# A hybrid layer (gated DeltaNet, RG-LRU, SwiGLU) in fp32 on one core: another order of the start, of the decay and of the recurrent steps

## The chip, the cores and the metric

One core of one Trainium2 chip. The metric is the device time of one execution in microseconds, the median of several runs. The kernel works in fp32 throughout; there is one launch.

## What is computed

```python
proj = x @ w_in                                   # x: 512 x 1024, 8720 columns
q, k, v, z, b_raw, a_raw, lru_x, lru_g, gate_dn, gate_lru = jnp.split(proj, IN_SPLIT_IDX, axis=-1)
qkv = jax.nn.silu(causal_depthwise_conv(jnp.concatenate([q, k, v], axis=-1), dn_conv_w))
...
beta = jax.nn.sigmoid(b_raw.astype(jnp.float32))
g = -jnp.exp(dn_A_log) * jax.nn.softplus(a_raw + dn_dt_bias)
o = gated_delta_rule_chunked(q, k, v, g, beta)    # 8 heads of 128, chunks, a triangular solve per chunk
...
u = causal_depthwise_conv(lru_x, lru_conv_w) + lru_conv_b
h = rg_lru(u, lru_w_a, lru_b_a, lru_w_i, lru_b_i, lru_lambda)     # 10 blocks of 128
y_lru = (h * jax.nn.gelu(lru_g)) @ w_branch_lru
merged = g_dn * y_dn + g_lru * y_lru
return merged @ w_out
```

Behind it follow a residual with layer norm, a SwiGLU with 2816 hidden columns, and a second residual with layer norm.

## The kernel before

Every large product is made of three matmuls of 512 columns (mm3, L154): weights and data are split into a high and a low part, and high x high, high x low and low x high are added in PSUM. The high part is a cast on ACT, the low part a subtraction on DVE or GpSimd (split, L129; split_w, L173). Weights come in pieces of 128 columns over 8 blocks of 128 rows (load_w, L164, on SP's queue), so one piece is 24 matmuls. The projections are called pj (q, k, v, z), lx and lg (LRU input and gate) and g (merge gates).

**Start** (L184 to L280). SP loads x (tiles xc) and the first weights (tiles wk, columns of k and q of heads 0 and 1). ACT's queue issues the load of wba (the columns of b_raw and a_raw) and eight loads of small parameters into rw. PE transposes the blocks of x (xp, L245); ACT and DVE split them into xT. psba is the product for beta and the decay, 16 columns wide. `first` are the four products of the first weights, made behind all transposes and all of psba. ACT and DVE are in the written order there; afterwards a scheduler orders them, and `urgent()` (L96) raises the priority of what stands in it.

**Recurrence.** Four chains dn_chain (L475), one for two heads each, run between the projections. Their steps, by the names of their PSUM tiles: kt (k to token order), kk (k times k), qt, qk, vt, then the inversion of the triangular matrices on 16 x 16 to 128 x 128 blocks (m, and i in several steps; xa, Fl and Yf are its tiles, most of its work is on DVE), then per chunk ks, xr, su, and the outputs oa, ob. Five chains lru_chain (L802) make the gates of the LRU (lw, L807) and the recurrence: r and ig are its gates, a the factor, u the state, gl the gelu of lg. decay_chain (L349) makes beta and the cumulated decay from psba; through it every dn_chain must wait.

**What sets the order.** PE's order is written by a planner at build time. It has a clock that only counts PE's own work, and a table LAT (L23) of how long the other engines need behind each step:

```python
                    pe, lat = next(ch[1])
                    ch[0] = clock[0] + pe + lat
                    clock[0] += pe
```

advance (L290) takes a chain's next step once the clock is past ch[0]; otherwise the next three matmuls of a projection are issued. before_merge (L848) takes projections in the sequence ORDER, as soon as enough of 40 SBUF slots are free (slot, free, NEED, and room, L436, which makes a chain wait for slots). PSUM has eight banks in two rings (bank, L85): "d", five banks after the start, for the chains, and "p" for projections. A chain step takes the bank that was taken five takes earlier, and waits on the chip until that one's reader is done. conv (L423) reads a projection's bank with one pass on ACT and three on DVE.

**The end.** merge, w_out, a layer norm, the SwiGLU and its down product follow. The last product (L1205ff) has its blocks' banks in `tops`; `cc` are banks that the combined products used, and dl0 is a further bank of ring "p", which the sum into h read just before.

Of the kernel before, what the change touches and what calls it, by code (L numbers as in the profile page):

```python
# [22 lines left out]
LAT = {  # L23
    "F": 13.0, "kt": 12.0, "q": 5.2, "qk": 5.0, "P": 4.0, "vt": 2.0, "u": 10.0, "sub": 33.0, "m1": 7.0,
    "m2": 8.0, "i2": 6.0, "i4": 7.0, "i5": 7.0, "x": 8.0, "ks": 5.0, "xr": 7.0, "su": 6.5, "ot": 26.0,
    "ba": 9.0, "g": 2.5, "conv": 14.0,
}
# [6 lines left out]
P = 128  # L34
# [12 lines left out]
def layer_kernel(  # L47
# [159 lines left out]
    load_x(256, 256)  # L207
    load_x(512, 256)
    load_x(768, 256)
    for m in range(4):  # L210
        load_first(m)

# [3 lines left out]
    S.dma_start(out=wbav, in_=win[:, :, CB:CB + 16])  # L216
    rw = slot("rw")
    r1, r2 = rw[0:96, 0, 0:P], rw[0:97, 1, 0:P]
    S.dma_start(out=r1, in_=dn_conv_w[0].rearrange("k (n p) -> (k n) p", p=P))
    S.dma_start(out=r2[0:40, :], in_=lru_conv_w[0].rearrange("k (n p) -> (k n) p", p=P))  # L220
    for j, v in enumerate((lru_conv_b, lru_b_a, lru_b_i, lru_lambda)):
        S.dma_start(out=r2[40 + 10 * j:50 + 10 * j, :], in_=v[0].rearrange("(n p) -> n p", p=P))
    S.dma_start(out=r2[80:96, :], in_=b_merge_gate[0].rearrange("(n p) -> n p", p=P))
    S.dma_start(out=r2[96:97, :], in_=dn_norm_w)
# [25 lines left out]
    def split_first(m, j):  # L250
        if j == 0:
            ws.append([wp.tile([P, 1024], F32R, tag=t, name=f"{t}f{m}") for t in ("wh", "wl")])
        split(*[t[:, T * j:T * j + T] for t in ws[m]], wk[m][:, j], V if m % 2 == 0 else G)
        if j == 1:
            free(wk[m])
# [6 lines left out]

    with tc.manual_schedule(engines={mybir.EngineType.Activation, mybir.EngineType.DVE}):
        for k in range(NK):
            transpose_x(k)
            if k == 1:
                n = NK * 16
                split(wbh[:, 0, 0:n], wbh[:, 1, 0:n], wba[:, 0, 0:n])
            if k >= 2:
                product_ba(k - 2)  # L270
            if k >= 6:
                split_first(0, k - 6)
        product_ba(6)
        product_ba(7)
    for t in xcs:
        free(t)
# [44 lines left out]
    def start(gen, lat):  # L321
        chains.append([clock[0] + lat, gen])

    def softplus(o, v, tmp):

        e, s2 = tmp
        act(e, v, AF.Abs)
        act(e, e, AF.Exp, scale=-1.0)
        V.tensor_scalar(out=s2, in0=e, scalar1=2.0, scalar2=None, op0=ALU.add)
        V.reciprocal(out=s2, in_=s2)  # L330
        tt(V, e, e, s2, ALU.mult)
        tt(V, s2, e, e, ALU.mult)
# [16 lines left out]
    def decay_chain():  # L349
# [452 lines left out]
    def lru_chain(p, u, r, ig, gw):  # L802
        n0 = 2 * p
        for g, (t, b) in enumerate(((r, 1), (ig, 2))):
# [8 lines left out]
        a, gl = slot(f"a{p}"), slot(f"gl{p}")  # L813
        gls[p] = gl
# [6 lines left out]
        stt(m, m, 1.0, r, ALU.add, ALU.mult)  # L821
        act(m, m, AF.Sqrt, bias=tiny)
# [9 lines left out]
        free(r, a, gl, ig)  # L832
# [38 lines left out]
    for n in range(4 * NK):  # L871

        k, i = (n // 4, n % 4) if n < 24 else (6 + n % 2, (n - 24) // 2)
        if n % 8 == 0 and n < 24:
            split_first(n // 8 + 1, 0)
            split_first(n // 8 + 1, 1)
        if n == 8:
            columns_of_parameters()
        wh, wl = [t.rearrange("p (j k c) -> p j k c", j=2, k=2) for t in ws[k // 2]]
        cs = slice((i % 2) * P, (i % 2) * P + P)  # L880
        mm3(first[i], wh[:, i // 2, k % 2, cs], wl[:, i // 2, k % 2, cs], xT[k][:, 0], xT[k][:, 1],
            k == 0, k == NK - 1)
        clock[0] += 0.68
        advance()
# [320 lines left out]
    for q, (name, right, banks, new, then) in enumerate(products):  # L1205
# [62 lines left out]
```

## Time and profile before

| | |
|---|---|
| median of three runs (lowest, highest) | 1018.65 us (1018.27, 1019.77) |
| the profiled execution, its own time and its span | 1017.21 us, 1015.5 us |
| PE busy, share of the span | 985.5 us, 97% |
| PE weight loads | 810.5 us, 80% |
| DVE | 621.8 us, 61% |
| ACT | 451.3 us, 44% |
| GpSimd (POOL) | 268.7 us, 26% |
| DMA | 128.52 MB, mean 127 GB/s |

The shares are means over the span: the DVE has 61% of it, but it is busy nearly all the time in some slices of the recurrence and little in others. Names like kt<-ident,x in the rows give the tile written and the tiles read, without their numbers; PEld is the load of weights into PE, which goes beside its matmuls. The trace lists a wait under the line of the instruction that waited, and behind the arrow what ended it.

### The profile page before, as it was taken

How to read it: one execution, taken by the hardware profiler on the slowest of the kernel's cores; microseconds unless marked ns; L12 is line 12 of the kernel's file. 1: busy time of each engine (PE TensorE's matmuls, PEld its weight loads, DVE VectorE, ACT ScalarE, POOL GpSimd, SP SyncE). 2: the span in 40 equal slices, each digit the busy share in tenths (PEclk: the TensorE clock that was granted, in tenths of full speed). 3: DMA queues.
4: the chain of work that ended last, by engine and by line, in shares of the span. 5: the costliest groups of instructions: out<-in, count | busy, mean ns of one | idle time of the engine just before them, and what ended most of it. 6: DMA issues, size and time to landing. Idle time of an engine off the chain costs nothing.

```text
span 1015.5 us, 14361 instructions
## 1 busy us (share of the span) xinstructions
PE 985.5 (97%) x5531; PEld 810.5 (80%) x5531; DVE 621.8 (61%) x1318; ACT 451.3 (44%) x619; POOL 268.7 (26%) x278
## 2 busy tenths in 40 slices
PE   7999999999999999999999999999999999999986
PEld 4887767777887888788888888798888888888875
DVE  3678999846777791265223464976344443388676
ACT  4598365359416743574322234322222222375451
POOL 2473534425343724265200003132000100000041
PEclk9999999999999999999999999999999999999998
DMA  8331322323222223234332527579354563346653
GB/s 255 105 104 53 84 74 63 84 73 84 64 63 73 75 66 89 63 112 127 103 94 84 171 88 207 187 268 327 110 163 154 181 207 90 97 136 195 194 188 107
DMA packets 161288, 128.52 MB, mean 127 GB/s; under 512 B 5499, under 2 KB 140860, under 8 KB 161220
## 3 DMA queue, kind: packets, MB, share of 16 engines
q1 hardware_dynamic: 152032, 99.12, 33.3%
q0 software_dynamic: 7872, 28.32, 7.5%
q8 instruction: 43, 0.70, 0.3%
q10 hardware_dynamic: 1316, 0.16, 0.1%
q14 instruction: 25, 0.20, 0.1%
HBM read 113.94 MB, written 13.65 MB: 126 GB/s over the span
## 4 chain that ended last, share of the span: by engine, by line
PE 75%; DVE 14%; ACT 4%; POOL 2%; issue 2%; DMA 1%; ACTq 0%; DVEq 0%; POOLq 0%
PE fu L157 4%; PE fg L157 4%; PE fg L155 4%; PE fu L155 4%; PE fu L156 4%; PE fg L156 4%; PE pj L155 3%; PE pj L156 3%; PE pj L157 3%; PE g L155 3%; PE g L157 3%; PE g L156 3%; DVE xa L121 3%; PE yl L157 2%; PE yl L156 2%
## 5 line engine op out<-in xcount | busy, mean ns | idle before, releaser
L135 ACT CAST wh<-wr 128x1024 fp32r<-128x1024 f32 (+1 forms) x163 | 168.5, 1034 | 363.2 <-PE fg L156 74.3
L121 POOL TENSOR_TENSOR wl<-wr,wh 128x512 fp32r<-128x512 f32 x128 | 172.4, 1369 | 216.0 <-ACT wh L135 211.5
L121 DVE TENSOR_TENSOR wl<-wr,wh 128x1024 fp32r<-128x1024 f32 x99 | 120.1, 1215 | 113.0 <-ACT wh L135 112.9
L155 PE MATMUL pj<-xT,wh 128*128 128x512 f32 x224 | 91.9, 410 | 0.0
L157 PE MATMUL pj<-xT,wl 128*128 128x512 f32 x224 | 87.5, 391 | 0.0
L156 PE MATMUL pj<-xT,wh 128*128 128x512 f32 x224 | 87.4, 390 | 0.0
L127 ACT ACT_TABLE_LOAD x62 | 79.5, 1283 | 12.4 <-DMA rw<-in_lru_conv_w 6.9
L155 PE MATMUL fg<-hk,wh 128*128 128x512 f32 x160 | 62.3, 389 | 0.0
L156 PE MATMUL fg<-hk,wh 128*128 128x512 f32 x160 | 62.3, 389 | 0.0
L157 PE MATMUL fg<-hk,wl 128*128 128x512 f32 x160 | 62.2, 389 | 0.0
L155 PE MATMUL fu<-hk,wh 128*128 128x512 f32 x160 | 62.2, 389 | 0.0
L156 PE MATMUL fu<-hk,wh 128*128 128x512 f32 x160 | 62.2, 389 | 0.0
L157 PE MATMUL fu<-hk,wl 128*128 128x512 f32 x160 | 62.2, 389 | 0.0
L155 PE MATMUL g<-xT,wh 128*128 128x512 f32 x128 | 51.1, 399 | 0.0
L157 PE MATMUL g<-xT,wl 128*128 128x512 f32 x128 | 50.0, 391 | 0.0
L156 PE MATMUL g<-xT,wh 128*128 128x512 f32 x128 | 49.9, 390 | 0.0
L124 DVE SCALAR_TENSOR_TENSOR x<-pj,cols,x 128x511 f32<-128x511 f32 (+2 forms) x60 | 44.5, 742 | 8.6 <-ACT x L127 8.2
L157 PEld LDWEIGHTS pj<-xT,wl 128*128 128x128 f32 x224 | 42.0, 188 | 9.1
L155 PEld LDWEIGHTS pj<-xT,wh 128*128 128x128 f32 x224 | 42.1, 188 | 7.9
L121 POOL TENSOR_TENSOR h<-h,g 128x512 f32<-128x512 f32 x4 | 6.0, 1499 | 160.2 <-ACT h L127 160.2
L156 PEld LDWEIGHTS pj<-xT,wh 128*128 128x128 f32 x224 | 42.2, 188 | 7.1
L121 DVE TENSOR_TENSOR xa<-xa 128x16 f32<-128x16 f32 (+14 forms) x116 | 37.6, 324 | 2.3
(387 smaller groups left out, 2366.2 us busy)
## 6 DMA issues: line engine op xcount, KB each, us to landing
wr<-in_w_in SPq DMA_DIRECT2D x64, 512.0 KB, 3.6
wr<-in_w_ffn_gate SPq DMA_DIRECT2D x22, 512.0 KB, 3.7
wr<-in_w_ffn_up SPq DMA_DIRECT2D x22, 512.0 KB, 3.7
b<-in_w_ffn_down POOLq DMA_DIRECT2D x22, 512.0 KB, 5.2
td<-b POOLq DMA_DIRECT2D x22, 512.0 KB, 4.0
wr<-td SPq DMA_DIRECT2D x20, 512.0 KB, 3.7
wr<-in_w_ffn_down SPq DMA_DIRECT2D x15, 512.0 KB, 3.4
wr<-in_w_branch_lru SPq DMA_DIRECT2D x8, 512.0 KB, 3.4
```

The lines of the kernel that those rows point to most:

```text
L121: return eng.tensor_tensor(out=o, in0=a, in1=b, op=op)
L124: return V.scalar_tensor_tensor(out=o, in0=a, scalar=s, in1=b, op0=op0, op1=op1)
L127: return S.activation(out=o, in_=i, func=func, **kw)
L135: S.copy(out=hi, in_=src)
L155: PE.matmul(ps, wh, rh, start=start, stop=False, **kw)
L156: PE.matmul(ps, wh, rl, start=False, stop=False, **kw)
L157: PE.matmul(ps, wl, rh, start=False, stop=stop, **kw)
```

## The change

Five parts. (1) SP's queue alternates blocks of x and first weights; the eight small loads go from ACT's queue to SP's, behind them. In the start PE makes, for each block of x, the transposes, then the previous block's psba product and its four first products; all low parts of the first weights are made on DVE. (2) beta comes from an exponential, an addition and a reciprocal instead of the sigmoid, the absolute value in softplus from DVE; the decay's operations have high priority. (3) lru_chain takes its slots r, ig and a when its gates begin, and waits for room then; gl takes r's place. (4) Thirteen planned latencies are longer. (5) The last product's first block has the bank cc[0].

```diff
-    "F": 13.0, "kt": 12.0, "q": 5.2, "qk": 5.0, "P": 4.0, "vt": 2.0, "u": 10.0, "sub": 33.0, "m1": 7.0,
-    "m2": 8.0, "i2": 6.0, "i4": 7.0, "i5": 7.0, "x": 8.0, "ks": 5.0, "xr": 7.0, "su": 6.5, "ot": 26.0,
-    "ba": 9.0, "g": 2.5, "conv": 14.0,
+    "F": 13.0, "kt": 13.5, "q": 5.2, "qk": 5.5, "P": 4.5, "vt": 2.0, "u": 10.0, "sub": 33.0, "m1": 8.5,
+    "m2": 9.5, "i2": 7.0, "i4": 7.5, "i5": 7.5, "x": 8.5, "ks": 6.0, "xr": 7.5, "su": 7.0, "ot": 26.0,
+    "ba": 13.0, "g": 2.5, "conv": 14.0,
...
-    load_x(256, 256)
-    load_x(512, 256)
-    load_x(768, 256)
-    for m in range(4):
-        load_first(m)
-
     wba, wbh = slot("wba"), slot("wbah", F32R)
     wbav = wba[:, 0, 0:NK * 16].rearrange("p (k c) -> p k c", c=16)
     wbhv = wbh[:, :, 0:NK * 16].rearrange("p s (k c) -> p s k c", c=16)
     S.dma_start(out=wbav, in_=win[:, :, CB:CB + 16])
+    load_first(0)
+    for m in range(1, 4):
+        load_x(256 * m, 256)
+        load_first(m)
...
-    S.dma_start(out=r1, in_=dn_conv_w[0].rearrange("k (n p) -> (k n) p", p=P))
-    S.dma_start(out=r2[0:40, :], in_=lru_conv_w[0].rearrange("k (n p) -> (k n) p", p=P))
+    nc.sync.dma_start(out=r1, in_=dn_conv_w[0].rearrange("k (n p) -> (k n) p", p=P))
+    nc.sync.dma_start(out=r2[0:40, :], in_=lru_conv_w[0].rearrange("k (n p) -> (k n) p", p=P))
...
-        split(*[t[:, T * j:T * j + T] for t in ws[m]], wk[m][:, j], V if m % 2 == 0 else G)
+        split(*[t[:, T * j:T * j + T] for t in ws[m]], wk[m][:, j])
...
+        transpose_x(0)
+        n = NK * 16
+        split(wbh[:, 0, 0:n], wbh[:, 1, 0:n], wba[:, 0, 0:n])
+        for k in range(1, NK):
             transpose_x(k)
-            if k == 1:
-                n = NK * 16
-                split(wbh[:, 0, 0:n], wbh[:, 1, 0:n], wba[:, 0, 0:n])
-            if k >= 2:
-                product_ba(k - 2)
-            if k >= 6:
-                split_first(0, k - 6)
-        product_ba(6)
-        product_ba(7)
-    for t in xcs:
-        free(t)
+            if k % 2 == 1:
+                split_first(k // 2, 0)
+                split_first(k // 2, 1)
+                free(xcs[k // 2])
+            product_ba(k - 1)
+            for i in range(4 if k < NK - 1 else 0):
+                product_first(k - 1, i)
+        product_ba(NK - 1)
...
-        act(e, v, AF.Abs)
+        stt(e, v, -1.0, v, ALU.mult, ALU.max)
...
-        act(beta, psb3[:, :, 0:8], AF.Sigmoid)
-        tt(V, ga, psb3[:, :, 8:16], dtb[:, None, :].to_broadcast([P, 4, H]), ALU.add)
-        softplus(gg, ga, (e1, e2))
-        act(nA, nA, AF.Exp)
-        stt(gg, gg, -1.0, nA[:, None, :].to_broadcast([P, 4, H]), ALU.mult, ALU.mult)
+        with urgent():
+            tt(V, ga, psb3[:, :, 8:16], dtb[:, None, :].to_broadcast([P, 4, H]), ALU.add)
+            softplus(gg, ga, (e1, e2))
+            act(nA, nA, AF.Exp)
+            stt(gg, gg, -1.0, nA[:, None, :].to_broadcast([P, 4, H]), ALU.mult, ALU.mult)
+
+            act(beta, psb3[:, :, 0:8], AF.Exp, scale=-1.0)
+            V.tensor_scalar(out=beta, in0=beta, scalar1=1.0, scalar2=3e38, op0=ALU.add, op1=ALU.min)
+            V.reciprocal(out=beta, in_=beta)
...
-    def lru_chain(p, u, r, ig, gw):
+    def lru_chain(p, u, gw):
         n0 = 2 * p
+        yield from room(3)
+        r, ig, a = slot(f"r{p}"), slot(f"ig{p}"), slot(f"a{p}")
...
-        a, gl = slot(f"a{p}"), slot(f"gl{p}")
-        gls[p] = gl
...
+        gls[p] = gl = r
...
-    for n in range(4 * NK):
-
-        k, i = (n // 4, n % 4) if n < 24 else (6 + n % 2, (n - 24) // 2)
-        if n % 8 == 0 and n < 24:
-            split_first(n // 8 + 1, 0)
-            split_first(n // 8 + 1, 1)
-        if n == 8:
-            columns_of_parameters()
-        wh, wl = [t.rearrange("p (j k c) -> p j k c", j=2, k=2) for t in ws[k // 2]]
-        cs = slice((i % 2) * P, (i % 2) * P + P)
-        mm3(first[i], wh[:, i // 2, k % 2, cs], wl[:, i // 2, k % 2, cs], xT[k][:, 0], xT[k][:, 1],
-            k == 0, k == NK - 1)
-        clock[0] += 0.68
-        advance()
+    columns_of_parameters()
+
+    for i in range(4):
+        for k in (6, 7):
+            product_first(k, i)
+            clock[0] += 0.68
+            advance()
...
-            tops = [[(0, bankp("dl0"))], [(0, bankd("dl1")[:, 0:256]), (256, bankd("dl2")[:, 0:256])]]
+            tops = [[(0, cc[0])], [(0, bankd("dl1")[:, 0:256]), (256, bankd("dl2")[:, 0:256])]]
```

product_first(k, i) is the body of the removed loop: mm3 into first[i] with the weights of block k.

What moves, first on **ACT, at the start** (whf are high parts of the first weights, wbah those of wba, nA a parameter of the decay). Before:

```order
L223 DMA rw<-in_b_merge_gate 16x128
L224 DMA rw<-in_dn_norm_w 1x128
L127 ACT_TABLE_LOAD
L127 ACTIVATE nA<-nA 128x8
L130 CAST xT_132<-xp_127 128x512
L130 CAST xT_140<-xp_135 128x512
L130 CAST wbah<-wba 128x128
L130 CAST xT_150<-xp_145 128x512
L130 CAST xT_161<-xp_156 128x512
L130 CAST xT_172<-xp_167 128x512
```

With the change:

```order
L210 DMA wba<-in_w_in 128x8x16
L127 ACT_TABLE_LOAD
L127 ACTIVATE nA<-nA 128x8
L130 CAST xT_132<-xp_127 128x512
L130 CAST wbah<-wba 128x128
L130 CAST xT_142<-xp_137 128x512
L130 CAST whf_145<-wk_91 128x512 x2
L130 CAST xT_171<-xp_166 128x512
L130 CAST xT_194<-xp_189 128x512
L130 CAST whf_197<-wk_95 128x512 x2
```

The DMA issues are gone but one, and behind every second cast of a block of x stand the casts of its weights.

Second **DVE, in the inversion of chain 0**, from the readers of kk on (ig and r belong to LRU pair 0, x_0 is the convolution of v). Before:

```order
L124 SCALAR_TENSOR_TENSOR Fl_457<-kk_0_681,br_597,Fl_457 128x128 x4
L124 SCALAR_TENSOR_TENSOR Fl_457<-kk_1_690,br_597,Fl_457 128x128 x4
L594 TENSOR_SCALAR xa_562<-xa_562,up 128x128
L124 SCALAR_TENSOR_TENSOR xa_562<-xa_562,low 128x128
L121 TENSOR_TENSOR xa_562<-xa_562 128x8
L600 STREAM_SHUFFLE xa_562<-xa_562 128x8x2
L121 TENSOR_TENSOR xa_562<-xa_562 128x8x2 x2
L600 STREAM_SHUFFLE xa_562<-xa_562 128x8x3
```

With the change:

```order
L124 SCALAR_TENSOR_TENSOR Fl_540<-kk_0_796,br_679,Fl_540 128x128 x4
L124 SCALAR_TENSOR_TENSOR Fl_540<-kk_1_805,br_679,Fl_540 128x128 x4
L124 SCALAR_TENSOR_TENSOR ig_708<-ig_708,r_707 128x1024
L124 SCALAR_TENSOR_TENSOR x_0_610<-pj_0_0_777,cols,x_0_610 128x511
L606 TENSOR_SCALAR xa_644<-xa_644,up 128x128
L124 SCALAR_TENSOR_TENSOR x_0_610<-pj_0_0_777,cols,x_0_610 128x510
L124 SCALAR_TENSOR_TENSOR xa_644<-xa_644,low 128x128
L124 SCALAR_TENSOR_TENSOR x_0_610<-pj_0_0_777,cols,x_0_610 128x509
L121 TENSOR_TENSOR xa_644<-xa_644 128x8
L612 STREAM_SHUFFLE xa_644<-xa_644 128x8x2
```

Operations of LRU pair 0 and of the convolution now stand between the readers of kk and the inversion's first steps.

Third **PE, at the gate products lw of LRU pair 1**, where chain 0 is in its inversion and chain 2 begins. Before:

```order
L669 MATMUL i_1461<-xa_562 32x32 x2
L671 MATMUL i_1462<-xa_562 32x32
L807 MATMUL lw_0_0_1490<-u_1016,gr_1019 128x512
L155 MATMUL lg_1_1451<-xT_161,wh_1255 128x512
L156 MATMUL lg_1_1451<-xT_161,wh_1255 128x512
L157 MATMUL lg_1_1451<-xT_161,wl_1256 128x512
```

With the change:

```order
L497 MATMUL kt_0_1309<-ident,x_2_769 128x128 x4
L497 MATMUL kt_1_1317<-ident,x_2_769 128x128 x4
L155 MATMUL lg_1_1293<-xT_194,wh_1146 128x512
L156 MATMUL lg_1_1293<-xT_194,wh_1146 128x512
L157 MATMUL lg_1_1293<-xT_194,wl_1147 128x512
L645 MATMUL m_1347<-xa_644 32x16 x16
L821 MATMUL lw_0_0_1367<-u_964,gr_965 128x512
L155 MATMUL lg_1_1293<-xT_223,wh_1146 128x512
L156 MATMUL lg_1_1293<-xT_223,wh_1146 128x512
L157 MATMUL lg_1_1293<-xT_223,wl_1147 128x512
L645 MATMUL m_1347<-xa_644 32x16 x16
```

Before, kt of chain 2 and two steps i of chain 0 came ahead of lw; now kt stands close to it, with the step m in the place where i was.

## Rows read from the trace of the kernel before

**Rows 1.** Waits of PE on other engines: us in total, times, longest us
```profile
PE dl L155 <- DVE h L124: 2.7, 1, 2.7
...
PE i L660 <- DVE vb L121: 2.0, 1, 2.0
...
PE m L633 <- DVE Fl L124: 1.6, 1, 1.6
...
PE ks L708 <- DVE Fl L725: 1.3, 1, 1.3
...
PE ks L708 <- DVE Fl L124: 1.3, 1, 1.3
...
PE kk L542 <- DVE rkb L121: 1.0, 1, 1.0
...
PE i L669 <- DVE xa L664: 0.9, 1, 0.9
...
PE m L633 <- DVE xa L627: 0.6, 1, 0.6
```

**Rows 2.** Windows: busy us of each engine, granted PE clock, DMA share, GB/s
```profile
100.00:130.00 30.00, 28.45 (x272) 22.55 (x272) 28.98 (x76) 14.33 (x20) 18.66 (x24) 0.94 0.29 78
```

**Rows 3.** Timeline of PE, start: start us, us, engine line op [idle before <-releaser]
```profile
9.63 0.61 PE L155 MATMUL psba<-xT,wbah 128*16 128x512 f32 x1 [1.18 <-ACT wbah L130]
...
20.41 0.40 PE L155 MATMUL first<-xT,whf 128*128 128x512 f32 x1
...
21.10 0.39 PE L155 MATMUL first<-xT,whf 128*128 128x512 f32 x1
...
43.80 0.39 PE L155 MATMUL pj<-xT,wh 128*128 128x512 f32 x1
```

**Rows 4.** Timeline of ACT and POOL, start; last, the landing of tile nA
```profile
6.92 1.28 ACT L127 ACT_TABLE_LOAD   x1 [6.92 <-DMA rw<-in_lru_conv_w]
...
8.33 1.05 ACT L130 CAST xT<-xp 128x512 fp32r<-128x512 f32 x2
...
1.37 0.69 POOL L227 DMA_DIRECT2D nA<-in_dn_A_log  x1 [0.36 <-issue]
...
DMA to landing us min/median/max: 4.5/4.5/4.5
```

**Rows 5.** Tile wk, first weights: duration ns min/median/max, first and last start us
```profile
L130 ACT CAST whf<-wk x8: 614/622/631, 17.5 to 27.0; 128x512 fp32r<-128x512 f32 x8
...
L121 DVE TENSOR_TENSOR wlf<-wk,whf x4: 681/774/1615, 18.3 to 22.3; 128x512 fp32r<-128x512 f32 x4
```

**Rows 6.** Page, part 5: loads of ACT's tables, busy us, mean ns
```profile
L127 ACT ACT_TABLE_LOAD x62 | 79.5, 1283 | 12.4 <-DMA rw<-in_lru_conv_w 6.9
```

**Rows 7.** Timeline of PE: kk of chain 0, gate products of LRU pair 1
```profile
71.23 1.95 PE L542 MATMUL kk<-x 128*128 128x128 f32 x16
...
138.54 1.10 PE L807 MATMUL lw<-u,gr 128*128 128x512 f32 x2
```

**Rows 8.** Timeline of DVE between the same two places
```profile
72.65 2.15 DVE L124 SCALAR_TENSOR_TENSOR Fl<-kk,br,Fl 128x128 f32<-128x128 f32 x8
...
77.83 1.41 DVE L594 TENSOR_SCALAR xa<-xa,up 128x128 f32<-128x128 f32 x1 [3.04 <-POOL xa L593]
...
137.75 0.69 DVE L121 TENSOR_TENSOR kd<-kt,fl 128x512 f32<-128x512 f32 x1
```

**Rows 9.** Groups by form on DVE, 72 to 190 us: busy us, mean ns
```profile
L121 DVE TENSOR_TENSOR u<-u,ig 128x1024 f32<-128x1024 f32 x2 | 2.4, 1220 | 0.3 <-ACT ig L127 0.3
...
L124 DVE SCALAR_TENSOR_TENSOR ig<-ig,r 128x1024 f32<-128x1024 f32 x2 | 2.8, 1378 | 0.0
...
L124 DVE SCALAR_TENSOR_TENSOR x<-pj,cols,x 128x510 f32<-128x510 f32 x9 | 6.7, 741 | 0.1
```

**Rows 10.** Timeline of DVE and PE in the last product
```profile
991.86 2.77 DVE L121 TENSOR_TENSOR wl<-wr,wh 128x1024 fp32r<-128x1024 f32 x2
...
993.55 0.50 PE L156 MATMUL dl<-wl,a 128*128 128x512 f32 x1 [0.76 <-DVE wl L121]
```

More of the change, by code (lines that the diff above doesn't have):

```diff
@@ L216, in layer_kernel @@
     S.dma_start(out=wbav, in_=win[:, :, CB:CB + 16])
+    load_first(0)
+    for m in range(1, 4):
+        load_x(256 * m, 256)
+        load_first(m)
     rw = slot("rw")
     r1, r2 = rw[0:96, 0, 0:P], rw[0:97, 1, 0:P]
-    S.dma_start(out=r1, in_=dn_conv_w[0].rearrange("k (n p) -> (k n) p", p=P))
-    S.dma_start(out=r2[0:40, :], in_=lru_conv_w[0].rearrange("k (n p) -> (k n) p", p=P))
+    nc.sync.dma_start(out=r1, in_=dn_conv_w[0].rearrange("k (n p) -> (k n) p", p=P))
+    nc.sync.dma_start(out=r2[0:40, :], in_=lru_conv_w[0].rearrange("k (n p) -> (k n) p", p=P))
     for j, v in enumerate((lru_conv_b, lru_b_a, lru_b_i, lru_lambda)):
-        S.dma_start(out=r2[40 + 10 * j:50 + 10 * j, :], in_=v[0].rearrange("(n p) -> n p", p=P))
-    S.dma_start(out=r2[80:96, :], in_=b_merge_gate[0].rearrange("(n p) -> n p", p=P))
-    S.dma_start(out=r2[96:97, :], in_=dn_norm_w)
+        nc.sync.dma_start(out=r2[40 + 10 * j:50 + 10 * j, :], in_=v[0].rearrange("(n p) -> n p", p=P))
+    nc.sync.dma_start(out=r2[80:96, :], in_=b_merge_gate[0].rearrange("(n p) -> n p", p=P))
+    nc.sync.dma_start(out=r2[96:97, :], in_=dn_norm_w)
     nA = const.tile([P, H], F32, name="nA")
@@ L261, in product_ba, with product_first @@
         mm3(psba[0:16], wbhv[:, 0, k], wbhv[:, 1, k], xT[k][:, 0], xT[k][:, 1], k == 0, k == NK - 1)
+    def product_first(k, i):
+        wh, wl = [t.rearrange("p (j k c) -> p j k c", j=2, k=2) for t in ws[k // 2]]
+        cs = slice((i % 2) * P, (i % 2) * P + P)
+        mm3(first[i], wh[:, i // 2, k % 2, cs], wl[:, i // 2, k % 2, cs], xT[k][:, 0], xT[k][:, 1],
+            k == 0, k == NK - 1)
     with tc.manual_schedule(engines={mybir.EngineType.Activation, mybir.EngineType.DVE}):
-        for k in range(NK):
+        transpose_x(0)
+        n = NK * 16
+        split(wbh[:, 0, 0:n], wbh[:, 1, 0:n], wba[:, 0, 0:n])
+        for k in range(1, NK):
             transpose_x(k)
-            if k == 1:
-                n = NK * 16
-                split(wbh[:, 0, 0:n], wbh[:, 1, 0:n], wba[:, 0, 0:n])
-            if k >= 2:
-                product_ba(k - 2)
-            if k >= 6:
-                split_first(0, k - 6)
-        product_ba(6)
-        product_ba(7)
-    for t in xcs:
-        free(t)
+            if k % 2 == 1:
[6 more added lines that the diff above has]
+        product_ba(NK - 1)
     free(wba, wbh)
@@ L366, in decay_chain @@
         PE.matmul(psg[:, 0:32], tri, gg.rearrange("p c h -> p (c h)"), start=True, stop=True)
-        V.tensor_copy(out=gc.rearrange("p c h -> p (c h)"), in_=psg[:, 0:32])
-        V.tensor_scalar(out=ngc, in0=gc, scalar1=-1.0, scalar2=None, op0=ALU.mult)
-        act(egc, gc, AF.Exp)
+        with urgent():
+            V.tensor_copy(out=gc.rearrange("p c h -> p (c h)"), in_=psg[:, 0:32])
+            V.tensor_scalar(out=ngc, in0=gc, scalar1=-1.0, scalar2=None, op0=ALU.mult)
+            act(egc, gc, AF.Exp)
         yield 0.2, LAT["g"]
@@ L773, in lru_pair @@
         n0 = 2 * p
-        u, r, ig = slot(f"u{p}"), slot(f"r{p}"), slot(f"ig{p}")
+        u = slot(f"u{p}")
         gw = wg.tile([P, 4, P], F32, tag="gr" if p % 2 else "gs", name=f"gr{p}")
@@ L781, in then_u @@
             if j == 1:
-                start(lru_chain(p, u, r, ig, gw), LAT["u"])
+                start(lru_chain(p, u, gw), LAT["u"])
         keep = []
@@ L831, in lru_chain @@
         tt(V, h, h, gl, ALU.mult)
-        free(r, a, gl, ig)
+        free(r, a, ig)
         hs[p] = h
```

## Prediction, made before the result was known

> **What bounds the kernel now.** I read the list of TensorE's waits first. PE is busy 97% of the span, so time can only be won from its waits, from stretches at half clock, and from the tail. The reader should see in [rows 1] that nearly every wait is on the DVE and lies in the recurrent chains (m, i, kk, ks): 1.6, 0.9, 1.0, 0.6, 1.3, 2.0 and 1.3 us, 8.7 us in all, plus 2.7 us in the last product (dl). Then the windows: between 100 and 130 us the DVE is busy 28.98 of 30 us [rows 2], as busy as PE. So these waits have two possible causes: an order that plans a step too early, or a DVE that is full. The change treats the first; whether it helps hangs on the second. The granted clock of 0.94 in that window is a stretch at 1.2 instead of 2.4 GHz behind the 1.6 us wait, worth 30 x 0.06 = 1.8 us. Last come the start, where PE's products begin at 20.41 us and the first projection at 43.80 us [rows 3], and the end.
>
> **Start.** ACT's first work is a table load at 6.92, behind nine DMA issues, and its first cast comes at 8.33 [rows 4]. The eight parameter loads leave its queue; it then waits for nA, issued at 1.37 and landed 4.5 us later, 5.9. The casts start 2.4 us earlier, and so do the products of ba (9.63 before [rows 3]). With weights interleaved, products start then too instead of at 20.41. Against this, every second block now waits for its own weights: behind the cast of x, ACT needs 0.62 for the high half and DVE 0.68 for the low one [rows 5], with a cast of 0.53 (1.05 for two [rows 4]) ahead: 1.8 us after the transposes, where PE has one ba product and two matmuls of its own (five matmuls of 0.23, from 0.69 for three [rows 3]), 1.15. That is 0.7 in each of blocks 3 and 5; the last ba product waits about as long for its x, 2.1 together. The whole start moves by -2.4 to +0.5; I take -0.5, near the end at which the waits come in full, since ACT and DVE run strictly in the written order there. The half clock at the start (0.61 us for a matmul of ba against 0.40 later) stays.
> The Trainium skill, "DMA: Bandwidth & Descriptors", section Issuing engines are not separate DMA queues, says that all DMAs run on the same 16 engines, and that issuing from another one saves only sequencer time, usually small beside the transfer. By it the start would be worth nothing and the sum 0.5 higher; the trace shows ACT's sequencer held for 6.92 us, which is not small here.
> SP now issues the eight loads behind x and the first weights, so the weights of pj come some us later; pj needs them only at 43.80 and hides that. POOL loses four low halves, the DVE gains four (0.68 each, 2.7 us) where it idles. Nothing of this is on the path.
>
> **Decay.** The four added DVE operations have 32 or 10 columns and run where the DVE idles. ACT's table loads fall: 62 loads at 1.28 [rows 6] become 52, 12.8 us of ACT's time; no wait in [rows 1] is on ACT, so I count nothing (bounds 0 and -1). But the ba product now ends with the block loop, and with it the decay some 10 us later: chain 0's kk, at 71.23 before [rows 7], comes at about 84 (pj at 43.3, then 162 projection matmuls of 0.23 and four lw of 0.9), while PE fills in projections.
>
> **The chains.** Longer latencies and the late start put each chain step behind more projection work: 0.5 to 2.7 us more at most of the places of [rows 1]. If PE's plan were the limit, all waits there would go. But the DVE starts its chain work with kk, and it was already late by then. I compare the stretch from kk of chain 0 to the gate products of LRU pair 1 (lw). Before: PE went from 71.23 to 138.54, 67.3 us [rows 7], in it two waits of 1.6 and 0.9. The DVE worked from 72.65 to 138.44 [rows 8], 65.8 us, ending with kd<-kt of chain 2, whose bank lw takes. Now PE has 36 matmuls of 512 columns less there (168 instead of 204: 36 x 0.23 = 8.2 us), two lw (1.10 at most each [rows 7], I take 0.9) and the 25 small i products (0.9) less: 10.9 us less. The DVE's rows up to the same kd<-kt are almost the same, 165 for 170: without one u<-u,ig of 1.22 [rows 9], the other differences being 0.4 to 1 us of both signs, together 0.6 less. And the 3.04 us for POOL's xa [rows 8] shrink by an ig product (1.38) and a convolution pass (0.74 [rows 9]) that now stand there, 2.1. So the DVE needs 65.8 - 1.8 - 2.1 = 61.9 us; from PE's start of kk, 1.4 + 61.9 = 63.3. PE without the 10.9 us would be at that place at 67.3 - 10.9 = 56.4. It is **6.9 us later** for the same work, through waits of about 9.4 us where 2.5 were. About half should show at the first place, the value transposes (vt) of chain 0: they take the bank of qk, whose reader stands behind all of pair 0's recurrence and six convolution passes, while PE has 78 products (17.9 us) and six small steps between kk and vt. Bounds of this term: -4.3 (the waits and the half clock gone, no new ones) and +9 (nothing of POOL's wait covered). I take +6.5, close to the rows.
> Behind it, waits of 1.0, 0.6, 1.3, 2.0 and 1.3 [rows 1] were there before; as PE is now later against the DVE, and planned with more work between steps, I take them as gone: -6.2 (bounds 0 and -6.2). New ones: the last two steps of chain 0's inversion, with more DVE work ahead of them, and chain 2's first i product, which now has fewer rows ahead than before; each between 0 and 2.0, the largest of its kind [rows 1]; I take 0.75 each: +1.5.
>
> **Late LRU slots** decide when a projection or a gate product finds its slots; what that does to PE's order is in the counts above. **The last product's bank.** The 2.7 us wait on h goes, but the DVE's order there is unchanged: the low halves of the next weights run from 991.86 to about 993.24 and PE waits for them until 993.55 [rows 10]. Starting earlier it waits there instead: 0 (bounds 0 and -2.7).
>
> **Sum.** -0.5 + 6.5 - 6.2 + 1.5 = +1.3 on the profiled execution's 1017.2, or 1018.5. That execution lies 1.4 under the median of the three runs, so 1020.0 us against 1018.65. A measurement can tell about 0.2%, 2 us; this is no change.
>
> **Rivals.**
> A, faster: the DVE isn't the limit: its rows fall into gaps that it had (POOL's 3.04 us, 1.0 us of that window), and the planned distances win. Then 8.7 and 1.8 go with 0.5 of the start: 11 us, 1007.7; half of it, the likelier size, 1013.5. For it: each waiting place has more PE work ahead. Against: 28.98 of 30 us [rows 2]. Chance 0.28, of which 0.26 faster.
> B, slower: the DVE's backlog isn't worked off behind lw. The inversion's steps i4 and i5 of chain 0 have two pairs' recurrences ahead of them, so each late step again makes PE wait. Place: PE's i products about 155 to 180 us. Price: 2.0 for each of two steps, and once more a half-clock stretch of 1.8 behind a wait of 4 us or more: 1020 + 4.0 + 1.8 - 1.5 = 1024.3. It decides once the DVE is over 1 us late at i4. Chance 0.25, nearly all slower.
> The Trainium skill, "TensorE: Matmul & The Clock Gate", section HAM oscillation — how this bites in real kernels, says that idle gaps bring PE back to 1.2 GHz; the trace agrees behind the 1.6 us wait. By it both new waits would each cost 1.8, which is B's clock term and more.
> C, the change doesn't act: the longer latencies and the interleaved start cancel within 0.5 us and old waits return at the new places; 1018.7. Chance 0.10, same.
>
> **How the numbers follow.** The forecast has 0.37; its own range, 1016.5 to 1023, comes from the bounds of the chain terms: 0.25 same, 0.10 slower, 0.02 faster. With the rivals: faster 0.28, same 0.38, slower 0.34. The range 1013 to 1025 leaves out the better half of A and the ends of B.
>
> **What would show it.** Right: ba and first products from about 7 to 9 us, pj at 43.3; kk of chain 0 near 84; a PE wait of 3 to 6 us at vt of chain 0 near 107 us, another near lw of pair 1, both on DVE; fewer waits behind; the wait on h in dl replaced by one on wl. Wrong: no PE wait over 2 us between 84 and 150 us means A; waits at i of chain 0 after 155 us mean B; pj before 41 us means that the start was undervalued.

## The result, and the profile after

The changed kernel takes 1056.15 us, median of four runs (1054.41 to 1056.95), against 1018.46: a ratio of 1.0368, interval 1.0348 to 1.0387. It is 37.7 us slower. The forecast, 1020.0 with a range up to 1025, was wrong.

The profiled execution has a span of 1055.2 us. Its page, part 1 (busy us, share of the span, instructions of each engine):

```profile
PE 999.2 (95%) x5531; PEld 819.3 (78%) x5531; DVE 633.2 (60%) x1326; ACT 437.5 (41%) x607; POOL 254.3 (24%) x274
```

PE has the same 5531 matmuls as before and is busy 13.7 us longer, and it is idle 56.0 us instead of 30.0. So of the 39.7 us by which the span grew, 26 are waits, and some 14 are the same matmuls at a lower clock: the mean granted clock fell from 0.995 to 0.981 of 2.4 GHz.

The list of PE's waits after (total us, times, longest), answering to [rows 1]:

```profile
PE pj L155 <- ACT r L127: 17.5, 4, 7.9
...
PE lw L821 <- issue: 4.8, 1, 4.8
...
PE dc L156 <- DVE wl L121: 3.4, 2, 2.2
...
PE ks L720 <- DVE Fl L124: 2.9, 2, 2.5
...
PE g L155 <- ACT r L127: 2.9, 1, 2.9
...
PE psg L377 <- DVE c L340: 1.9, 1, 1.9
...
PE vt L497 <- DVE F L121: 1.5, 1, 1.5
...
PE vt L497 <- ACT x L127: 1.4, 1, 1.4
```

The first line was not in the kernel before at all: a projection waits four times for ACT's writing of r, 17.5 us, and the merge gates once more, 2.9. This is the gelu of lg, which the change puts into r.

Comparing the start of the same-numbered large matmul (lines L155 to L157) in two traces tells where the time is lost. The numbers count from 0; in us against the kernel before:

```
matmul number        100    300    500    800   1100   1400   1700
before, at          39.3   94.7  161.1  263.6  362.4  444.8  517.8
after               -3.4   +7.1  +16.2  +14.8  +27.0  +37.8  +38.2
E1, own slot        -2.6   -2.1  +11.7   +9.8  +16.8  +22.7  +23.2
E2, only r's reuse  -0.3   +9.8  +18.4  +19.0  +25.3  +34.6  +34.6
E3, no LRU part     -1.8   -1.3  +11.6  +11.3  +18.3  +24.2  +24.7
E16, decay 8.2 late -0.4   +7.1  +13.2  +13.1  +13.1  +13.1  +13.1
E19, decay 10.2 l.  -0.6   +9.6  +19.6  +18.1  +19.4  +19.5  +19.5
E11, decay late     -1.6   +8.8  +13.0  +18.0  +20.4  +24.3  +23.8
E6, latencies       -0.4   +1.3   +6.4   +9.1   +8.5  +13.5  +14.0
E9, decay part      -1.6   -1.6   +0.2   +0.1   +0.1   +0.2   +0.2
E15, E9 and loads   -2.1   -2.0   -1.9   -0.4   -0.4   -0.4   -0.4
```

Nearly all of the changed kernel's loss arises between 60 and 480 us, in the recurrence; what follows adds 1.5 us. The start is 3.4 us ahead. It went as its timeline says (start us, us, engine, line, op):

```profile
6.24 0.61 PE L155 MATMUL psba<-xT,wbah 128*16 128x512 f32 x1 [0.19 <-ACT wbah L130]
...
7.61 0.63 PE L155 MATMUL first<-xT,whf 128*128 128x512 f32 x1
...
8.32 0.39 PE L157 MATMUL first<-xT,wlf 128*128 128x512 f32 x1
...
41.02 0.39 PE L155 MATMUL pj<-xT,wh 128*128 128x512 f32 x1
```

Products begin at 7.61 instead of 20.41 and the projections at 41.02 instead of 43.80 [rows 3]; PE is at full clock from about 8.1 us on, where the kernel before reached it at about 15.4. The gain of 2.8 us is lost by 100 us.

**The wait on r.** PE, DVE and ACT around 90 us of the changed kernel, from their timelines:

```profile
96.26 0.79 PE L155 MATMUL pj<-xT,wh 128*128 128x512 f32 x1 [7.87 <-ACT r L127]
...
96.85 0.63 PE L156 MATMUL pj<-xT,wh 128*128 128x512 f32 x1
...
92.82 2.05 DVE L124 SCALAR_TENSOR_TENSOR ig<-ig,r 128x1024 f32<-128x1024 f32 x1 [1.84 <-ACT ig L127]
...
92.70 0.67 ACT L127 ACTIVATE x<-pj,cols 128x512 f32<-128x512 f32 x1
...
93.27 1.03 ACT L135 CAST wh<-wr 128x1024 fp32r<-128x1024 f32 x1
...
94.32 1.28 ACT L127 ACT_TABLE_LOAD   x1
...
95.61 1.08 ACT L127 ACTIVATE r<-lg 128x512 f32<-128x512 f32 x2
```

The gelu of lg (95.61) may not write r before the DVE has read it in ig<-ig,r. That operation began at 92.82 after a wait for ACT's square and ended at 94.87, and a convolution's first pass, a cast and a table load had come in between on ACT. lg's last matmul began at 79.85; ACT was busy without a pause from then on, most of it with the same pair's gates, which must all come before. Until the gelu has read lg's two banks, two of the three banks of ring "p" are not free, and the projection that needs the next one stands still for 7.87 us. Behind the wait its matmuls take 0.63 us, half clock.

The windows of 60 to 85 and 85 to 105 us (busy us of PE, weight loads, DVE, ACT, POOL, granted clock), after and then before:

```profile
60.00:85.00 25.00, 25.00 (x108) 19.41 (x107) 11.86 (x29) 20.63 (x38) 11.94 (x10) 1.00 0.52 149
...
85.00:105.00 20.00, 12.13 (x58) 9.93 (x57) 14.02 (x39) 19.38 (x29) 7.75 (x9) 0.83 0.19 53
```

```profile
60.00:85.00 25.00, 25.00 (x124) 19.95 (x123) 20.29 (x66) 20.28 (x37) 14.83 (x16) 1.00 0.33 92
...
85.00:105.00 20.00, 19.97 (x103) 16.76 (x102) 19.37 (x68) 19.57 (x23) 6.20 (x6) 1.00 0.21 55
```

Between 60 and 85 us, up to kk of chain 0, the DVE is busy 8.4 us less than in the kernel before. This half of the forecast holds: kk came at 85.07 (about 84 was forecast).

### The profile page after: what moved, and what is told of

Its sections match the earlier page's. It is cut to its first block, busy times and chain, and to the rows that moved or that the text cites. A ratio compares the mean times of both kernels' runs of the same rounds, so it can differ in the third digit from the quotient of the medians.

```text
span 1055.2 us, 14352 instructions
## 1 busy us (share of the span) xinstructions
PE 999.2 (95%) x5531; PEld 819.3 (78%) x5531; DVE 633.2 (60%) x1326; ACT 437.5 (41%) x607; POOL 254.3 (24%) x274
## 4 chain that ended last, share of the span: by engine, by line
PE 74%; DVE 17%; ACT 5%; issue 2%; DMA 1%; POOL 1%; SPq 0%; DVEq 0%; ACTq 0%; POOLq 0%
PE fg L157 3%; PE fu L156 3%; PE fg L156 3%; PE fu L157 3%; PE fg L155 3%; PE fu L155 3%; DVE xa L121 3%; PE pj L155 3%; PE pj L156 3%; PE pj L157 3%; PE g L155 3%; DVE x L124 3%; PE g L156 3%; PE g L157 3%; PE yl L156 2%
## 5 line engine op out<-in xcount | busy, mean ns | idle before, releaser
L121 POOL TENSOR_TENSOR wl<-wr,wh 128x512 fp32r<-128x512 f32 x128 | 167.3, 1328 | 253.5 <-ACT wh L135 243.5
L155 PE MATMUL pj<-xT,wh 128*128 128x512 f32 x224 | 94.4, 421 | 17.5 <-ACT r L127 17.5
L156 PE MATMUL pj<-xT,wh 128*128 128x512 f32 x224 | 90.1, 402 | 0.0
L157 PE MATMUL pj<-xT,wl 128*128 128x512 f32 x224 | 89.8, 401 | 0.0
L155 PEld LDWEIGHTS pj<-xT,wh 128*128 128x128 f32 x224 | 43.6, 195 | 27.7 <-ACT r L127 18.9
L155 PE MATMUL fg<-hk,wh 128*128 128x512 f32 x160 | 62.3, 389 | 0.0
L157 PE MATMUL fg<-hk,wl 128*128 128x512 f32 x160 | 62.3, 389 | 0.0
L155 PE MATMUL fu<-hk,wh 128*128 128x512 f32 x160 | 62.3, 389 | 0.0
L157 PE MATMUL fu<-hk,wl 128*128 128x512 f32 x160 | 62.3, 389 | 0.0
L155 PE MATMUL g<-xT,wh 128*128 128x512 f32 x128 | 52.7, 411 | 2.9 <-ACT r L127 2.9
L157 PEld LDWEIGHTS pj<-xT,wl 128*128 128x128 f32 x224 | 43.7, 195 | 9.5
L157 PE MATMUL g<-xT,wl 128*128 128x512 f32 x128 | 50.6, 396 | 0.0
L156 PE MATMUL g<-xT,wh 128*128 128x512 f32 x128 | 50.6, 395 | 0.0
L156 PEld LDWEIGHTS pj<-xT,wh 128*128 128x128 f32 x224 | 43.5, 194 | 8.0 <-issue 0.2
L121 DVE TENSOR_TENSOR xa<-xa 128x16 f32<-128x16 f32 (+14 forms) x116 | 42.5, 366 | 2.6
```

Of the source, the lines that this page charges most:

```text
L121: return eng.tensor_tensor(out=o, in0=a, in1=b, op=op)
L155: PE.matmul(ps, wh, rh, start=start, stop=False, **kw)
L156: PE.matmul(ps, wh, rl, start=False, stop=False, **kw)
L157: PE.matmul(ps, wl, rh, start=False, stop=stop, **kw)
```

## The experiments

Eighteen kernels ran. Medians stand against the kernel before on the same chip (1017.9 to 1019.1).

### First question: the reuse of r, or the order

E1: the changed kernel with

```diff
-        yield from room(3)
-        r, ig, a = slot(f"r{p}"), slot(f"ig{p}"), slot(f"a{p}")
+        yield from room(4)
+        r, ig, a, gl = slot(f"r{p}"), slot(f"ig{p}"), slot(f"a{p}"), slot(f"gl{p}")
...
-        gls[p] = gl = r
+        gls[p] = gl
```

> The changed kernel, but the gelu of lg goes into a slot of its own (four slots taken late instead of three). Theory R (reuse): gelu may not write r before the DVE has read it (ig<-ig,r, behind a square on ACT), and till then lg's PSUM banks are held and the next projection waits: 7.9, 3.1, 3.6, 2.9 and 2.9 us, 20.4 in all, each with a half-clock stretch behind it. Then these five waits vanish and the time falls by 20 to 34 us, to 1022 to 1036. Theory O (order): the late slots and longer latencies put PE's steps in a worse order against a full DVE, and the waits at r are only where it shows; then waits of the same sum appear elsewhere and the time stays above 1045.

Measured: 1044.1 us, 1.026 (1.024 to 1.028). The waits on r are gone and 12 us with them, but 26 us against before remain. That lies between the two theories: the list of waits has new entries.

```profile
PE m L634 <- DVE xa L622: 6.9, 1, 6.9
...
PE kt L497 <- ACT sq L127: 4.5, 1, 4.5
...
PE qk L571 <- ACT sq L127: 3.2, 2, 2.7
...
PE vt L497 <- DVE xa L121: 3.1, 1, 3.1
...
PE ks L720 <- DVE Fl L124: 3.0, 2, 2.5
...
PE su L734 <- DVE xa L729: 2.1, 1, 2.1
```

These are at 138.8 (m), 106.3 (kt), 119.9 (vt), 211.7 (qk), 334.8 (ks) and 216.3 us (su).

E2: the kernel before with gl in r and nothing else.

```diff
-        a, gl = slot(f"a{p}"), slot(f"gl{p}")
-        gls[p] = gl
+        a = slot(f"a{p}")
...
+        gls[p] = gl = r
```

> The kernel before with one edit: gelu of lg goes into r, no slot gl. Theory R: waits of a projection on ACT's r appear at the LRU pairs, 15 us or more in all, and the time is 1035 to 1055. Theory O: within 5 us of 1018.5, since order, start and latencies are those of before.

Measured: 1053.46 us, 1.0334 (1.031 to 1.0359). This one edit costs 35 us in the kernel before. PE's order is unchanged in it; only DVE, ACT, GpSimd and the loads come in another. PE's waits:

```profile
PE pj L155 <- ACT r L127: 17.7, 4, 8.3
...
PE g L155 <- ACT r L127: 6.6, 1, 6.6
...
PE i L669 <- DVE xa L664: 5.6, 2, 4.8
```

In the table above its loss grows around these five waits, one for each LRU pair, and around the longest one at i (148.3 us).

E3: the changed kernel with the whole LRU part undone.

> The changed kernel with the whole LRU part (late slots and gl in r) undone; start, decay, latencies and last bank stay. Theory R: no waits on r; the start's 3.4 us stay gained; between 1010 and 1025. Theory O, if the latencies or the start make the order bad: above 1035. If E1 and this differ by over 5 us, the late slots have an effect of their own.

Measured: 1043.06 us, 1.0243 (1.0227 to 1.0258). Theory R said 1010 to 1025 and fails as the only cause; theory O's condition, above 1035, is met. E1 and E3 lie 1 us apart, so late slots alone have no effect here that can be told.

E18: the kernel before with late slots, four of them, gl in its own.

> The kernel before with the LRU's four slots taken late and gl in a slot of its own: the other half of the LRU part, E2 (gl in r, early slots) cost 35 us. If E2's cost is the reuse, this is within 3 us of 1018, though its order differs after the first pair. Theory N: 1028 or more.

Measured: 1019.18 us, 0.9999 (0.999 to 1.0008). On no engine does the order differ from that of before, so the late slots by themselves move nothing in this kernel, and the reuse is what costs in the LRU part. Against expectation this kernel is no trial of theory N, whether another order costs by being another.

### Second question: start, decay or latencies

E4: the changed kernel with the LRU part and the latencies undone.

> The changed kernel with the LRU part and the longer latencies undone: start, decay and last bank are left. After E3 (1043.1) about 25 us have a cause other than r's reuse. Theory S (start): psba now ends with the block loop, the decay and chain 0 come over 10 us later, the DVE idles first and is late afterwards; then this stays near E3, 1035 to 1048. Theory L (latencies): the new planned distances make the order that waits; then it falls to 1010 to 1022.

Measured: 1037.78 us, 1.0184 (1.0166 to 1.0203), in theory S's range. Against E3 the longer latencies are missing, and 5 us with them.

E9: the kernel before with the decay part alone.

> The kernel before with the decay part alone (beta from an exponential, the absolute value on DVE, high priority). It removes ten table loads of ACT. Theories S and L: within 3 us of 1018. Theory D (decay): its priority reorders ACT and DVE ahead of chain 0, and this alone costs 10 us or more.

Measured: 1018.31 us, 1.0003 (0.9994 to 1.0013). Nothing, though it is 1.6 us ahead until 100 us (table above): the waits behind take it back. Only two of the ten table loads go here (62 to 60).

E10: the kernel before with the start (and the last bank) alone.

> The kernel before with the start alone (and the last bank, which E8 showed to be worth nothing). Theory S: 1030 to 1048; first products at about 7.5 us, kk of chain 0 near 84 us, DVE waits of PE from 100 us on. Theories L and D: 1013 to 1021, the 3.4 us of the start gained.

Measured: 1041.93 us, 1.0224 (1.0206 to 1.0242), theory S. E4 has the decay part besides and is 4 us faster: with the late start that part is worth something, though alone (E9) it is not.

E11: the kernel before with its old start, only

```diff
-    start(decay_chain(), 0.0)
+    start(decay_chain(), 16.3)
```

> The kernel before, but the planner starts the decay chain 16.3 us of PE's clock later (24 product groups of 0.68), as the new start does; the start itself, the loads and the latencies are those of before. Theory S (a late chain 0 leaves the DVE idle first and behind afterwards): 1030 to 1048, waits of PE on the DVE from 100 us on. Theory S2 (something else in the new start, its loads or its DVE splits, costs the time): within 4 us of 1018.

Measured: 1040.52 us, 1.0219 (1.0204 to 1.0234), the same as E10, and with the same waits; between the start and the last product PE's order is that of E10, too. PE's waits of E10 and then of E11:

```profile
PE psg L373 <- DVE dk L124: 7.3, 1, 7.3
...
PE vt L492 <- DVE kd L121: 4.4, 1, 4.4
...
PE su L729 <- DVE xa L724: 4.2, 1, 4.2
...
PE lw L814 <- DVE vb L121: 3.5, 1, 3.5
```

```profile
PE psg L366 <- DVE dk L124: 7.2, 1, 7.2
...
PE vt L485 <- DVE kd L121: 4.5, 1, 4.5
...
PE su L722 <- DVE xa L717: 4.2, 1, 4.2
...
PE lw L807 <- DVE vb L121: 3.5, 1, 3.5
```

So what the new start costs comes with the decay's later place in the plan, which alone costs as much; the loads and the splits, which E11 doesn't have, aren't needed for it. The first of these waits is direct. The decay's small operations now fall among convolution passes, as the DVE's timeline of E11 shows:

```profile
42.33 4.68 DVE L124 SCALAR_TENSOR_TENSOR x<-first,cols,x 128x511 f32<-128x511 f32 x7 [0.32 <-ACT x L127]
...
46.93 0.18 DVE L121 TENSOR_TENSOR dk<-psb,dtb 128x32 f32<-128x32 f32 x1
...
51.88 3.99 DVE L124 SCALAR_TENSOR_TENSOR dk<-dk 128x32 f32<-128x32 f32 x9
```

psb was made at 38.88, the decay's first operation runs at 46.93, and PE reaches psg and waits 7.2 us. The high priority of the decay part shortens that a little, as E4 shows:

```profile
PE psg L377 <- DVE c L340: 6.0, 1, 6.0
```

It falls to 1.9 us only with the longer latencies (E3, E1 and the changed kernel), where ba puts psg 4 us later in the plan.

E16 and E19: the same edit with 8.2 and 10.2 instead of 16.3.

> The kernel before with the decay started 8.2 us later in the planner. PE's order changes in some 300 rows, but kk of chain 0 stands only 3 rows (0.7 us) later. Theory S (lateness costs): within 3 us of 1018. Theory N (the order of before is a selected one, any other costs 10 us or more): 1028 or more.

> As E16 with 10.2 us: kk of chain 0 stands 12 rows (2.7 us) later, between E16 (3 rows) and E11 (30 rows, 22 us slower). Theory S: between the two, 1021 to 1033. Theory N: no relation to the lateness.

Measured: E16 1028.37 us, 1.0094 (1.0079 to 1.0109), E19 1035.57, 1.0163 (1.0149 to 1.0177). E16 is slower than theory S allowed and falls into theory N's range; E19 lies above the range of theory S. But E16's order is hardly another one: by the names in the traces, 108 of PE's 5531 matmuls stand at another place, where some 300 rows were expected. By PE's rows kk is 0.7 us later, but on the chip it is 7.3, since psr, the decay's next step behind psg, waits for the DVE:

```profile
49.65 1.01 PE L373 MATMUL psr<-ident,dk 128*8 128x128 f32 x4 [4.21 <-DVE dk L367]
```

By kk's real time the series is in line:

```
                   kk of chain 0   DVE busy 60 to 85 us   ratio to before
before                  71.23             20.29              1
E18, late slots         71.48             20.22              0.9999
E16, decay 8.2 late     78.48             15.55              1.0094
E19, decay 10.2 late    83.75             16.26              1.0163
E10, new start          88.94             13.63              1.0224
E11, decay 16.3 late    89.97             12.67              1.0219
E4, start and decay     87.72             14.62              1.0184
E3, no LRU part         86.71             11.90              1.0243
E21, step latencies     70.94             20.29              1.0058
E20, ba and kt          72.39             18.00              1.0072
E6, all latencies       72.92             17.54              1.0141
E14, latencies shorter  75.59             18.18              1.0231
```

From before over E16 and E19 to E11, each microsecond by which kk comes later costs 1.2 to 1.3 us of the whole. Part of this is the direct wait on the decay, ahead of kk: 4.2 us in E16, 6.9 at psg in E19, 7.2 in E11, and at matmul 300 they are already 7.1, 9.6 and 8.8 us behind. The rest of these executions' loss, 6 to 15 us, arises later. That speaks for the lateness. That the new order of PE has a cost of its own beside it isn't excluded: in E19 and E11, 935 and 2157 matmuls stand elsewhere. And the latencies' rows at the end of the table don't follow the lateness: E14's kk comes 4.4 us later, and the whole takes some 24 us more.

### Third question: the latencies

E6: the kernel before with the thirteen new values of LAT.

> The kernel before with the thirteen longer latencies alone. Theory L: 1035 or more, with new waits between 100 and 230 us. Theory S: within 6 us of 1018, waits of chain steps fewer or smaller.

Measured: 1032.72 us, 1.0141 (1.0125 to 1.0157): 14 us, between the theories. Its largest new wait is 5.3 us, at lw of pair 1:

```profile
146.06 2.05 PE L807 MATMUL lw<-u,gr 128*128 128x512 f32 x2 [5.28 <-DVE u L124]
```

E14: the thirteen shortened by as much.

> The kernel before with the thirteen latencies shortened by as much as the change lengthens them. E6 (longer) cost 14 us. If the direction matters (later steps make the DVE late), shorter ones cost less than 5 us or even gain, waits being many and short. If the order of before is simply a selected one and any other costs, then 1028 or more, too.

Measured: 1042.76 us, 1.0231 (1.0215 to 1.0247), with 6.2 us at m, 3.2 at su and 3.0 at psg. Along this line of thirteen values, both directions cost, as the second theory had it. Why they do, no run shows.

E20: only ba 13 and kt 13.5. E21: only the other eleven.

> The kernel before with only two of the thirteen latencies longer, those ahead of kk of chain 0 (ba 9 to 13, kt 12 to 13.5). Theory S: E6's 14 us come mainly from a later chain 0; this costs 5 us or more, with kk later than 72 us. Rival: the steps inside the chains cost it, and this is within 3 us of 1018.

> The kernel before with the other eleven latencies longer, those of the steps inside the chains; kk of chain 0 stays at about 71 us. Theory S: within 4 us of 1018, waits at m, i and ks smaller. Rival: 1026 or more, since the longer distances delay the state steps and with them the banks.

Measured: E20 1026.52 us, 1.0072 (1.0046 to 1.0099); E21 1024.52, 1.0058 (1.0041 to 1.0076). The two groups share E6's cost about equally. E20 meets theory S's conditions, with kk 1.2 us later, but by the series above that much lateness is worth 1.5 us, not 7. Its waits are those of before, grown (PE's waits of E20; 0.9, 1.6 and 1.3 us in [rows 1]):

```profile
PE i L669 <- DVE xa L664: 5.3, 1, 5.3
...
PE m L633 <- DVE Fl L124: 3.6, 1, 3.6
...
PE ks L708 <- DVE Fl L725: 2.9, 1, 2.9
```

In E21 kk is on time (70.94) and the largest wait is 5.1 us, again at lw of pair 1; neither theory's range holds. Why longer distances lead to these waits was not settled.

### Last bank, loads, GpSimd, and a better version

E8: the kernel before with cc[0] as the last product's first bank.

> The kernel before, only the last product's first bank is cc[0]. The prediction: no gain, the wait of 2.7 us on h turns into one of about the same size on wl, 1018.0 to 1019.0. Rival: the 2.7 us go, 1015.8.

Measured: 1019.14 us, 1.0006 (0.9994 to 1.0017). No gain, as predicted: its two waits of 1.2 and 2.2 us at dc stand for those of 2.7 and 0.8 at dl. The changed kernel's trace shows why: the wait on h is gone [rows 1], PE starts earlier and waits for the low halves of the next weights (timelines of PE and DVE, after):

```profile
1027.88 0.51 PE L156 MATMUL dc<-wl,a 128*128 128x512 f32 x1 [1.18 <-DVE wl L121]
...
1033.20 0.50 PE L156 MATMUL dc<-wl,a 128*128 128x512 f32 x1 [2.21 <-DVE wl L121]
...
1031.52 2.76 DVE L121 TENSOR_TENSOR wl<-wr,wh 128x1024 fp32r<-128x1024 f32 x2
```

E12: the kernel before with the eight loads on SP's queue.

> The kernel before, with only the eight parameter loads moved from ACT's queue to SP's, behind x and the first weights; PE's and DVE's orders are unchanged. ACT's first cast comes some 2 us earlier. If the stretch from 72 to 190 us is bound by the DVE, the gain of 1 to 2 us there is taken back by the same waits: 1017 to 1019. If PE's path counted throughout, 1016 to 1017.

Measured: 1018.16 us, 0.9994 (0.9986 to 1.0002), not told from nothing. In the profiled executions 2.7 us were ahead at 92 us, and 0.9 are left: the first wait at m grew from 1.6 [rows 1] to 3.0.

```profile
116.08 0.44 PE L633 MATMUL m<-xa 32*32 32x16 f32 x32 [3.02 <-DVE Fl L124]
```

E13: the kernel before with h x gl on GpSimd.

> The kernel before, but the LRU's product h x gl (1.41 us on the DVE, five times) is made by GpSimd; PE's order is unchanged. If the full DVE sets PE's waits in the chains, these fall by 1 to 4 us and the time is 1014 to 1017. If they are set by the planned distances alone, within 1 us of 1018; if GpSimd slows the DVE beside it, above 1019.

Measured: 1020.66 us, 1.0027 (1.0018 to 1.0035), slower: the last of the three cases. What it shows of the DVE is told at the end.

E15: E9 and E12 together.

> The kernel before with the decay part and the eight loads on SP's queue together: the two parts that cost nothing alone (E9, E12), as a version that might beat it. PE's order is unchanged. E9 was 1.6 to 3.1 us ahead until 125 us, E12 1.2 us ahead after 160 us. If the full DVE takes it back, 1016.5 to 1019; if part stays, 1014 to 1016.5.

Measured: 1017.71 us against 1019.05, 0.9988 (0.9979 to 0.9997). This version is the fastest of all, by some 1.2 us over the kernel before, which is at the edge of what these runs can tell; it is made of two parts of the change without its start, its reuse, its latencies.

## Why the prediction was wrong

The parts added one after the other give the account: the start alone costs 24 us (E10), with the decay part 20 (E4), with the latencies 25 (E3), and with the LRU part 38 (the changed kernel). The prediction had +1.3 for the first three together and nothing for the LRU part. So two steps failed: the chain terms (+6.5, -6.2, +1.5), which put a late chain 0 at +1.8 in all, and the reuse of r, which had no term.

**Late LRU slots.** This step failed. The prediction took the part as one of slots and order, with its effect "in the counts above", and put no price on gl in r. It names no rival for it either. But here a buffer that is reused is a wait: the gelu has to come behind the last reader of r, and what stands behind the gelu is lg's PSUM bank and the next projection. The edit costs 35 us alone (E2) and 12 us on top of the rest (E1 against the changed kernel). That it is less there because PE stands still in the chains anyway is a guess that no run tries.

**Chains up to lw**, +6.5 us. The mechanism was right, the size too small: chain 0 later, the DVE idle first and full afterwards, new waits of PE in the chains. kk came at 85.07, and lw of pair 1 waited 4.83 us. The profile names no releaser for it, but kd<-kt, which the prediction expected there, had ended 0.1 us before (PE and DVE, after):

```profile
154.87 2.01 PE L821 MATMUL lw<-u,gr 128*128 128x512 f32 x2 [4.83 <-issue]
...
154.08 0.68 DVE L121 TENSOR_TENSOR kd<-kt,fl 128x512 f32<-128x512 f32 x1
```

vt of chain 0, where 3 to 6 us were forecast on the DVE, waited only 1.4 us, behind the long wait on r. Without the reuse, PE waited 4.5, 3.1 and 6.9 us at kt, vt and m between 100 and 140 us (E1), 14.4 where about 9.4 was forecast; the one at kt was on ACT, which the prediction had left out. At matmul 500, E1 and E3 are 11.7 and 11.6 us behind. The step was about half of what it should have been. It counted PE's rows at full clock; but the same matmuls ran longer behind the long waits.

**Behind lw**, -6.2 and +1.5. This step failed. The waits there were taken as gone because PE would be late. In E1 they were not gone: qk, vt, su and ks waited 9.4 us between 190 and 340, more than the 6.2 of before. A chain that starts 15 us late ends late, and in E1 the loss grows from 11.7 to 22.7 us between matmul 500 and 1400. Rival B had this in part: the waits at i that it placed at 155 to 180 us are there in E4, E10 and E11 (1.7, 1.0 and 1.2 us between 160 and 183, 3.8 us against its 4.0), but not in E1 or the changed kernel, and the waits behind them it didn't have.

**Latencies.** They were never costed by themselves; the prediction put them into one count with the start. Alone they cost 14 us (E6), on top of the late start 5 (E3 against E4). The view that a longer planned distance can only shorten a wait is refuted by E6, E20 and E21. What makes them cost stays open.

**Start**, -0.5. Sign right, size too small: pj is 2.8 us earlier in the changed kernel and 1.1 to 2.0 in E3, E4 and E1, which have the same start. The half clock at the start, taken as unchanged, ended 7 us earlier. The Trainium skill, "DMA: Bandwidth & Descriptors", section Issuing engines are not separate DMA queues, says that issuing from another engine saves only the sequencer's time, usually small beside the transfer. The prediction put the start at nothing by it. E12 shows 2.7 us won up to 92 us by moving eight issues off ACT's sequencer, so the trace decides; in the medians nothing of it can be told.

**Decay and last bank**, both 0: right for each alone (E9, E8); behind the late start the decay part is worth 4 us (E4 against E10). The ten table loads, which the prediction gave to the decay, go mostly with the reuse of r: E2 has 53 of 62, and E1, the change without the reuse, 61. A slip in rival A changes nothing: half of its 11 us is 1013.2, not 1013.5.

**The clock.** The stretches at 1.2 GHz behind idle gaps, which the prediction kept for rival B at 1.8 us, were some 14 us of the result. They should have been a term. But not every wait has one: in the changed kernel the seven longest waits in the recurrence (2.5 to 7.9 us) each have a stretch at half clock, in E1 only three of the six waits over 2 us there (those of 4.5, 6.9 and 2.1 us), and in the kernel before the waits of 2.0 and 2.7 us [rows 1] have none.

## What to carry to other kernels

A buffer reuse is priced as a wait: who reads the old content last, who writes the new, and what (a PSUM bank, an in-order queue) stands behind the writer. When a faster start makes the first link of a long dependent chain later, ask what that costs, even if PE has other work for the time: here up to 2.8 us were saved and some 20 lost, partly in waiting for the first link itself, partly later, when the engine that serves the chain, idle before, was full. How much of it the new order of PE costs by itself stays open. Price one part of a bundle at a time, and count a clock stretch to the longer waits.

## What the runs showed of the hardware

In E13 GpSimd's product held up the DVE. The timelines of both (E13):

```profile
107.90 2.40 POOL L121 TENSOR_TENSOR u<-u,gl 128x1024 f32<-128x1024 f32 x1
...
108.00 2.33 DVE L144 TENSOR_SCALAR rk<-rk 128x8 int32<-128x8 int32 x1
```

A DVE operation on 128 x 8 numbers took 2.33 us, until GpSimd's was over; in the kernel before the same operation (at 109.49) took 0.17. It happens there too: of 180 DVE operations on 128 x 8 numbers, 18 took 0.55 to 1.30 us, and each of these ended within 0.03 us of the end of a GpSimd operation. The Trainium skill, "SBUF — State Buffer", section SBUF: two separate sides, says that DVE and GpSimd have one port pair in common, which the first one holds for its whole instruction if the DVE's operation is in a mode that uses both of its ports, or reads two SBUF operands while GpSimd reads SBUF. The trace agrees that the DVE was held; which mode this operation runs in, no run shows. Such holds, and GpSimd's longer 2.46 us for each of the five products against 1.55 on the DVE, may be why taking 7.8 us of work off the DVE made the kernel 2.4 us slower; that was not tried.

Behind waits, the half-clock stretches cost half of what the waits cost in the changed kernel: 13.7 us more busy time beside 26 us more idle time. The share isn't fixed: it was 6.5 beside 18.1 us in E1, and 7.9 beside 7.8 in E6.
